# Input projection of a hybrid attention block: dense weights and tokens as fp16 halves with scales found on the chip

## The chip, the cores and the metric

The kernel runs on one core of one Trainium2 chip. The metric is the device time of one execution in microseconds (us). The kernel before has a median of 585.36 us over 2 runs (585.01 and 585.7).

The engines are named as in the profile: PE does matmuls and PEld its weight loads, DVE is VectorE, ACT is ScalarE, POOL is GpSimd, and SP issues the DMAs.

## The reference, cut to what matters

```python
D_MODEL, SEQ, N_META = 1024, 512, 16        # 528 tokens: 16 meta tokens, then 512
MLA_HEADS = FOX_HEADS = 16                  # both branches are 1024 wide
...
u = rmsnorm(h, pre_norm_g[l])
proj = u @ w_in[l]                          # [528, 1024] @ [1024, 7600]
(cq, ckv, k_pe_raw, z_mla, fq, fk, fv, f_logit, z_fox, gate_a, gate_b) = jnp.split(proj, split_idx, axis=-1)
...
y_mla = (o_mla * jax.nn.silu(z_mla)) @ w_br_mla[l]
...
o_fox = causal_block_attention(fox_heads(fq), fox_heads(fk), fox_heads(fv), FOX_SCALE, cum)
y_fox = (o_fox * jax.nn.silu(z_fox)) @ w_br_fox[l]
mixed = (jax.nn.sigmoid(gate_a) * y_mla + jax.nn.sigmoid(gate_b) * y_fox) @ w_out[l]
h = h + rmsnorm(mixed, post_norm_g[l])
```

The case is about `u @ w_in`: 7168 of its 7600 output columns are `z_mla`, `fq`, `fk`, `fv`, `z_fox` and the two gates. The other 432 (`cq`, `ckv`, `k_pe_raw`, `f_logit`) are the small projections.

## The kernel before, in words

**Three products for one.** Every fp32 matrix product is made of two parts per operand. A high part is the operand in the type fp32r, a low part is what the high part leaves, and three matmuls are summed in PSUM: high weights by high tokens, high weights by low tokens, low weights by high tokens. The tokens are `uTh` and `uTl` (1024 rows as 8 blocks of 128 partitions, 528 columns).

**Units.** The dense part of `w_in` is cut into 56 units of 128 output columns: 8 each of `fq`, `fk` and `v` (`fv`), 16 of `z` (8 for each branch) and 16 of `pg` (the gates). A unit has 8 blocks of the contraction and three products for each. `z`, `fq` and `pg` have 24 matmuls of 512 columns; `fk` and `v` also take the meta tokens and have 24 matmuls of 272 and 24 of 256 columns.

For each unit one DMA brings 128x1024 of raw fp32 weights (`wraw`, 512 KB). ACT casts the high part (`w<-wraw`, L136), and `split_lo` (L105) subtracts it from the raw weights for the low part, on POOL for 43 units of this size and on DVE for the others (`low[0]` names the engine).

**Stages.** After a preamble of some 59 us (tokens normed and transposed, small projections `psm`, first `fq` and `fk`) come 16 attention stages, one for two heads of a branch, FoX and MLA in turn; a FoX stage and the MLA stage after it are a pair here. Each stage computes scores (`st`), turns them on ACT and DVE into probabilities (`sf`, `pn`; L795, L830, L869), transposes these by DMA (`pt`), and multiplies them with the values of the stage before (`ov`). Between these PE works off a list called `fill`, which prepares the next stages:

- in a FoX stage (a z-stage below): the two `z` units of the pair, the first whole, the second in pieces between `mq`, `mk` and `v` of the next MLA stage;
- in an MLA stage (an fq-stage below): `fq`, `fk` and `v` of the next FoX stage.

PE's order is written out by hand (`tc.manual_schedule`). The other engines take an order from the tile framework's priorities, fixed when the program is built. After the last stage, at about 395 us, the merge begins: nine of the gates, the two branch projections and the output projection, with POOL idle.

**What consumes a unit.** `hl_done` (L251 on ACT, L105 on DVE) splits `fq` and `fk` into `hlq` and `hlk`. `z_unit` takes a tanh on ACT and L746 on DVE (`sil`). `v_unit` finds a scale for each partition (L710 to L720), and makes `vh`. `gate_unit` takes a tanh.

## Time and profile before

| what | value |
|---|---|
| median of the runs | 585.36 us (585.01, 585.7) |
| the profiled execution's own time | 585.71 us |
| its span, first to last instruction | 583.5 us |
| mean granted TensorE clock | 0.999 |
| busy time of PE, DVE, ACT, POOL | 574.2, 414.5, 356.4, 200.7 us |

The span has 2.2 us less than the execution's time. Busy time is a sum over stages that differ; a stage has to be read by its own window. A row of the timeline gives the start of an instruction in us from the span's start, its duration, engine, line, operation, output and inputs, shapes and a count, and in brackets the idle time before it and what ended that. A row of the groups gives the count, the busy time in us and the mean duration in ns. A matmul's duration reaches from its start until its last result is written, and the next matmul starts long before that, so the pace of PE is the distance of starts and not the duration.

### The profile page before, as it was taken

To read this page: it belongs to the slowest core of one execution; us is meant where nothing else is said; L and a number is where in the kernel's file an instruction comes from. 1 tells how busy PE (TensorE), PEld (TensorE's weight loads), DVE (VectorE), ACT (ScalarE), POOL (GpSimd) and SP (SyncE) were. 2 spreads that over 40 slices of the span, in tenths; PEclk is the share of its full clock that TensorE was granted. 3 is DMA by queue.
4 is the path that set the end of the run, shared out by engine and by line. 5 is a ranking of instruction groups with operands and counts; after the bars stand their busy time and mean duration, and the time that the engine had idled before them with its cause. 6 is when DMAs were issued, how large, how long until landed. Compare 5 with 4: busy or idle time off the path is not lost.

```text
span 583.5 us, 11105 instructions
## 1 busy us (share of the span) xinstructions
PE 574.2 (98%) x3841; PEld 496.5 (85%) x3841; DVE 414.5 (71%) x1156; ACT 356.4 (61%) x816; POOL 200.7 (34%) x270
## 2 busy tenths in 40 slices
PE   8999999999999999999999999999999999999995
PEld 6989889889889888888898898878998998888884
DVE  5854876884775775767758748895747876468967
ACT  7856774884774775767748747944343462443762
POOL 4317835464468472654544634520000000000000
PEclk9999999999999999999999999999999999999999
DMA  9535699999978999988987978977722534332603
GB/s 293 119 88 151 125 189 218 234 184 269 175 167 158 231 192 215 220 164 208 186 175 182 216 158 147 184 168 259 210 73 72 145 105 132 89 110 88 237 0 144
DMA packets 219999, 97.46 MB, mean 167 GB/s; under 512 B 131456, under 2 KB 209672, under 8 KB 219944
## 3 DMA queue, kind: packets, MB, share of 16 engines
q1 hardware_dynamic: 219944, 96.77, 71.2%
q8 instruction: 30, 0.49, 0.3%
q14 instruction: 25, 0.20, 0.1%
HBM read 62.36 MB, written 3.97 MB: 114 GB/s over the span
## 4 chain that ended last, share of the span: by engine, by line
PE 93%; ACT 2%; DMA 2%; issue 1%; POOL 1%; SPq 0%; DVE 0%; DVEq 0%; ACTq 0%; POOLq 0%
PE z L99 17%; PE pg L99 15%; PE v L99 9%; PE fk L99 8%; PE fq L99 8%; PE x L99 8%; PE py L99 7%; PE st L99 7%; PE ov L99 5%; PE psm L99 3%; PE y L99 2%; PE mq L99 2%; DMA pt<-pn 1%; PE ppe L99 1%; DMA wsr<-in_w_in_dram 1%; PE mk L99 1%
## 5 line engine op out<-in xcount | busy, mean ns | idle before, releaser
L105 POOL TENSOR_TENSOR w<-wraw,w 128x1024 fp32r<-128x1024 f32 (+2 forms) x61 | 118.6, 1951 | 113.8 <-ACT w L136 81.5
L136 ACT CAST w<-wraw 128x1024 fp32r<-128x1024 f32 (+1 forms) x72 | 74.6, 1041 | 48.5 <-PE py L99 19.7
L99 PE MATMUL z<-uTh,w 128*128 128x512 f32 x256 | 85.0, 393 | 0.0
L99 PE MATMUL pg<-uTh,w 128*128 128x512 f32 x256 | 80.7, 391 | 0.0
L830 ACT ACTIVATE sf<-sf,nb 128x272 f32<-128x272 f32 (+3 forms) x128 | 72.7, 569 | 11.5 <-DVE nb L795 10.6
L105 DVE TENSOR_TENSOR w<-wraw,w 128x512 fp32r<-128x512 f32 (+1 forms) x55 | 51.6, 949 | 27.9 <-ACT w L1125 20.0
L869 DVE SCALAR_TENSOR_TENSOR pn<-sf,ri,pn 128x512 f16<-128x512 f32 (+3 forms) x128 | 69.6, 609 | 1.6 <-ACT pn L865 1.5
L865 ACT ACTIVATE pn<-sf,ri 128x128 f16<-128x128 f32 (+3 forms) x128 | 59.7, 548 | 0.5 <-DVE ri L835 0.5
L99 PEld LDWEIGHTS pg<-uTh,w 128*128 128x128 f32 x256 | 48.1, 188 | 10.2 <-issue 0.3
L99 PEld LDWEIGHTS z<-uTh,w 128*128 128x128 f32 x256 | 48.1, 188 | 10.2
L99 PE MATMUL z<-uTl,w 128*128 128x512 f32 x128 | 50.1, 391 | 0.0
L99 PE MATMUL pg<-uTl,w 128*128 128x512 f32 x128 | 49.9, 390 | 0.0
L99 PE MATMUL fk<-uTh,w 128*128 128x272 f32 (+1 forms) x256 | 48.5, 283 | 0.0
L99 PE MATMUL v<-uTh,w 128*128 128x272 f32 (+1 forms) x256 | 47.5, 283 | 0.0
L99 PE MATMUL fq<-uTh,w 128*128 128x512 f32 x128 | 42.0, 398 | 0.0
L99 PE MATMUL st<-hlk,hlq 64*128 64x272 f32 (+4 forms) x480 | 41.2, 299 | 0.0
L710 DVE TENSOR_REDUCE vsc<-v 128x1 f32<-128x272 f32 (+1 forms) x32 | 13.2, 433 | 39.5 <-PE v L99 39.5
L99 PEld LDWEIGHTS fk<-uTh,w 128*128 128x128 f32 x256 | 40.4, 188 | 0.3
L99 PEld LDWEIGHTS v<-uTh,w 128*128 128x128 f32 x256 | 40.0, 188 | 0.1
L99 PE MATMUL py<-gh,w 128*128 128x512 f32 x128 | 39.7, 389 | 0.0
L99 PEld LDWEIGHTS st<-hlk,hlq 64*128 64x128 f32 x480 | 33.1, 186 | 4.1 <-ACT vh L729 2.8
L99 PE MATMUL v<-uTl,w 128*128 128x256 f32 (+1 forms) x128 | 36.2, 283 | 0.0
(255 smaller groups left out, 1332.1 us busy)
## 6 DMA issues: line engine op xcount, KB each, us to landing
wraw<-in_w_in_dram SPq DMA_DIRECT2D x56, 512.0 KB, 4.8
cbp<-c_dram SPq DMA_DIRECT2D x16, 264.0 KB, 4.0
wraw<-in_w_br_fox_dram SPq DMA_DIRECT2D x8, 512.0 KB, 4.2
tb<-in_w_out_dram SPq DMA_DIRECT2D x8, 512.0 KB, 5.4
wraw<-in_w_br_mla_dram SPq DMA_DIRECT2D x8, 512.0 KB, 4.2
wraw<-in_w_out_dram SPq DMA_DIRECT2D x6, 512.0 KB, 4.2
xr<-in_x_dram SPq DMA_DIRECT2D x4, 512.0 KB
out_dram<-yo SPq DMA_DIRECT2D x8, 256.0 KB, 2.0
```

The source lines that it names most:

```text
L99: nc.tensor.matmul(*a, **k)
L105: return eng.tensor_tensor(out=lo, in0=src, in1=f32(hi), op=ALU.subtract)
L136: nc.scalar.copy(wh[:, :n], raw[:, :n])
L710: nc.vector.tensor_reduce(out=sc[:, i : i + 1], in_=ps, op=ALU.max, axis=AX.X, apply_absolute_value=True)
L830: exps[b // 3] = nc.scalar.activation(sf, sf, AF.Exp, bias=sums["nb"][:, h, b : b + 1], scale=-1.0, accum_out=sums["su"][:, h, b : b + 1]).ins
L865: normed[:] = [nc.scalar.activation(hi, sf, AF.Copy, scale=rib).ins]
L869: nc.vector.scalar_tensor_tensor(out=lo, in0=sf, scalar=rib, in1=hi, op0=ALU.mult, op1=ALU.subtract)
```

## The change

**Tokens.** `pre_norm_g` is multiplied by a power of two from its largest magnitude, and the tokens are split into fp16 halves `hTh` and `hTl`. The factor is taken out again by constants in `su`, by which POOL also rescales `rt` and `gq` (128x320 and 128x384). The small projections still run as fp32r: for the first two token tiles POOL makes `hTh` and `hTl` from `uTh` and `uTl` (`narrowed`: a CAST of 128x1024 and two TENSOR_TENSOR of 128x1024 per tile), for the last two it makes `uTh` and a copy of `uTl` (`widened`: 8 CASTs of 128x512).

**Weights.** Each of the 56 units gets a scale. `peak` is a DVE reduction of the raw 128x1024 to a maximum of magnitude per partition. For each set of one to three units, a PE matmul of these maxima against a constant 128x128 tile (`spread`) gives a bound on every partition, and DVE takes the power of two out of it by bit operations (L195) and a reciprocal (L197), and POOL the factor back (L198). There are 24 such matmuls for the sets and one more for the tokens. Then ACT writes the high half with that scale (one instruction per unit, as the cast was). The low half is one DVE instruction for 10 units; for 46 units it is two POOL instructions, a TENSOR_SCALAR of raw times scale (L237, two operations, the second times 1.0) and the subtraction (L238).

**Consumers** undo the scales in instructions that were there already (an activation's scale, a `scalar_tensor_tensor` in place of a `tensor_tensor`), with two more 128x1 POOL instructions per stage.

**Order.** The units are built earlier, since a set's scale comes ahead of the first of its weights: a z-stage finds the scales of the three units `fq`, `fk`, `v` of the next fq-stage, an fq-stage those of the two `z` units of the next pair. Two buffers for raw weights are added, and loads are issued a stage earlier. `gT` and the sums of the merge move to rooms that the tokens leave.

```diff
-SC_FOX = 1.0 / math.sqrt(HD)
+SC_FOX = 4.0 / math.sqrt(HD)
...
+    spread = const.tile([128, 128], BF16, tag="spread", name="spread")
+    nc.gpsimd.memset(spread, 2.0 ** -14)
...
+    def scales(ws):
+        st = {}
+        def peak(j):
+            raw = ws[j].load()[1]
...
+            mp = st["sc"][:, 0:2].bitcast(BF16)[:, j : j + 1]
+            tc.keep_in_program_order(nc.vector.tensor_reduce(out=mp, in_=raw, op=ALU.max, axis=AX.X, apply_absolute_value=True))
+        def run_():
...
+            for w in ws:
+                w.peak()
+            sc, n = st["sc"], len(ws)
+            ps = scale_bank[0](f"scale{uid[0]}")[:, 0:n]
+            mm(ps, spread, sc[:, 0:2].bitcast(BF16)[:, 0:n], start=True, stop=True)
+            t, inv, r = (sc[:, o : o + n] for o in (3, 7, 11))
+            with tc.high_priority(offset=200):
+                nc.vector.tensor_scalar(out=t.bitcast(I32), in0=ps.bitcast(I32), scalar1=0x7F800000, scalar2=0x00800000,
+                                        op0=ALU.bitwise_and, op1=ALU.bitwise_or)
+                nc.vector.reciprocal(inv, t)
+                nc.gpsimd.tensor_scalar(out=r, in0=t, scalar1=su[:, 5:6], scalar2=1.0, op0=ALU.mult, op1=ALU.mult)
...
+    class Halved:
...
+        def __call__(self):
...
+            self.scale()
+            u, raw, parts, n = self.ld
...
+                nc.scalar.activation(hi, raw, AF.Copy, scale=self.s)
...
+                if low[0] is nc.vector:
+                    nc.vector.scalar_tensor_tensor(out=lo, in0=raw, scalar=self.s, in1=hi, op0=ALU.mult, op1=ALU.subtract)
+                else:
+                    whole_ = f32(room[:, 1024:2048])
+                    nc.gpsimd.tensor_scalar(out=whole_, in0=raw, scalar1=self.s, scalar2=1.0, op0=ALU.mult, op1=ALU.mult)
+                    nc.gpsimd.tensor_tensor(out=lo, in0=whole_, in1=hi, op=ALU.subtract)
...
     def u_act(k):
-        return uTh[:, k, :], uTl[:, k, :]
+        return hTh[:, k, :], hTl[:, k, :]
...
-    def win_w(off, i, up=0):
-        return weights(lambda: [win[:, :, off + 128 * i : off + 128 * i + 128]], lambda w: by_k(w[0], KD), up)
+    def win_w(off, i, room=None):
+        return Halved(lambda: win[:, :, off + 128 * i : off + 128 * i + 128], room)
...
-                za, zb = z_unit(1, pr), z_unit(0, pr)
-                fill = (vts[br, pr] if pr else begun) + za + q + zb[:3] + k + zb[3:5] + v + zb[5:]
+                za, zb = zs[pr]
+                q, k, v = feeds[si + 1]
+                fill = (vts[br, pr] if pr else begun) + za + q + zb[:3] + k + zb[3:5] + v + call(ws[0].scale, ws[0]) + zb[5:] + call(ws[1])
+                fill += loads_of(sets[si + 1])
...
-                fill = vts[br, pr] + q + k[:KD] + v + k[KD:]
+                    fill = vts[br, pr] + q + k[:KD] + v[:4] + call(ws[0].scale, ws[0]) + v[4:] + k[KD:] + call(ws[1]) + loads_of(sets[si + 1])
+                middles.append([sets[si - 1][2]])
...
                 n1()
+                for w in sets[si]:
+                    w.peak()
```

How this moves instructions on the engines is shown at three places. The first is DVE in a z-stage, after the scaled probabilities (`pn`). The row of numbers at the end is the output's shape. Before:

```order
L869 SCALAR_TENSOR_TENSOR pn_714<-sf_3161,ri_3159,pn_714 128x4x128
L746 SCALAR_TENSOR_TENSOR sil_3303<-sil_3303,z_3256 128x512
L105 TENSOR_TENSOR hlq_3320<-mq_3313,hlq_3320 128x512
L105 TENSOR_TENSOR hlk_3355<-mk_3351,hlk_3355 128x272
L105 TENSOR_TENSOR hlk_3355<-mk_3358,hlk_3355 128x256
L710 TENSOR_REDUCE vsc_3374<-v_3370 128x1
```

Now, at the same place (L1022 is the old L869, L897 the old L746, L855 the old L710):

```order
L1022 SCALAR_TENSOR_TENSOR pn_785<-sf_3333,ri_3331,pn_785 128x4x128
L182 TENSOR_REDUCE sc_3509<-wraw_3323 128x1
L897 SCALAR_TENSOR_TENSOR sil_3473<-sil_3473,z_3426 128x512
L182 TENSOR_REDUCE sc_3509<-wraw_3325 128x1
L109 TENSOR_TENSOR hlq_3489<-mq_3482,hlq_3489 128x512
L182 TENSOR_REDUCE sc_3509<-wraw_3327 128x1
L109 TENSOR_TENSOR hlk_3523<-mk_3519,hlk_3523 128x272
L109 TENSOR_TENSOR hlk_3523<-mk_3526,hlk_3523 128x256
L855 TENSOR_REDUCE vsc_3542<-v_3538 128x1
L195 TENSOR_SCALAR sc_3509<-scale_3560 128x3
```

Three peaks (L182) now stand between `pn` and `hlk`, and L195 reads what PE made of them.

The second place is PE in the same z-stage, after `v` of the MLA stage that follows and ahead of the last piece of the second `z` unit. Before:

```order
L99 MATMUL v_3376<-cTl,w_3306 128x256
L99 MATMUL v_3376<-cTh,w_3306 128x256
L99 MATMUL z_3329<-uTh,w_3324 128x512
L99 MATMUL z_3329<-uTl,w_3324 128x512
L99 MATMUL z_3329<-uTh,w_3324 128x512 x2
```

Now:

```order
L103 MATMUL v_3544<-cTl,w_3477 128x256
L103 MATMUL v_3544<-cTh,w_3477 128x256
L103 LDWEIGHTS spread
L103 MATMUL scale_3560<-sc_3509,spread 128x3
L103 LDWEIGHTS w_3319
L103 MATMUL z_3493<-hTh,w_3319 128x512
```

The scale matmul is new here; where `z` followed `v` directly, it now stands behind a matmul that reads the three peaks.

The third place is POOL between the end of a z-stage and the middle of the next fq-stage, where it makes the low parts of `fq`, `fk` and `v`. Before:

```order
L105 TENSOR_TENSOR w_3512<-wraw_3254,w_3512 128x1024
L105 TENSOR_TENSOR w_3569<-wraw_3311,w_3569 128x1024
L720 TENSOR_SCALAR vsc_3374<-vsc_3374 128x1
L105 TENSOR_TENSOR w_3623<-wraw_3327,w_3623 128x1024
L850 TENSOR_TENSOR mt_3587<-sf_3408,ri_3406 128x32
```

Now (L1003 is the old L850):

```order
L198 TENSOR_SCALAR sc_3509<-sc_3509,su 128x3
L237 TENSOR_SCALAR w_3565<-wraw_3323,sc_3509 128x1024
L869 TENSOR_SCALAR vsc_3542<-vsc_3542 128x1
L237 TENSOR_SCALAR w_3582<-wraw_3325,sc_3509 128x1024
L238 TENSOR_TENSOR w_3565<-w_3565 128x1024
L903 TENSOR_SCALAR vsc_3542<-sc_3185,vsc_3542 128x1
L237 TENSOR_SCALAR w_3735<-wraw_3327,sc_3509 128x1024
L238 TENSOR_TENSOR w_3582<-w_3582 128x1024
L238 TENSOR_TENSOR w_3735<-w_3735 128x1024
L1003 TENSOR_TENSOR mt_3766<-sf_3594,ri_3592 128x32
```

The low half of `fq` (`w_3565`) is finished by the fifth of these instructions, behind the first steps of `fq` and of `fk`; that of `fk` is finished after the first step of `v`.

## The prediction, as it was put on record

> **What bounds the kernel now.** I read the page first, then the chain of waits, then the groups by shape, and last the timeline of one pair of stages in the middle of the program.

> ```profile
> span 583.5 us, 11105 instructions
> PE 93%; ACT 2%; DMA 2%; issue 1%; POOL 1%; SPq 0%; DVE 0%; DVEq 0%; ACTq 0%; POOLq 0%
> ```

> ```profile
> 226.20:244.30 18.10, 18.10 (x123) 14.75 (x122) 14.47 (x57) 14.25 (x35) 7.93 (x11) 1.00 0.98 221
> 244.30:267.00 22.70, 22.70 (x197) 20.67 (x196) 14.23 (x48) 13.89 (x35) 12.73 (x19) 1.00 0.89 187
> 400.00:450.00 50.00, 50.00 (x308) 44.98 (x307) 30.27 (x47) 18.98 (x34) 0.00 (x0) 1.00 0.53 159
> ```

> ```profile
> PE psm L99 <- POOL wsh L306: 0.5, 1, 0.5
> ```

> The chain is PE for 93% of the span. The windows (after each window's length: PE, PEld, DVE, ACT, POOL, clock, DMA share, GB/s) show a z-stage, the fq-stage after it, and a piece of the merge. PE has no gap in any of them and a granted clock of 1.00. So the time is the sum of PE's steps, and the change counts in two ways: how much shorter a step becomes, and whether PE now has to wait. DVE is busy 14.47 of 18.10 us in the z-stage, the least room that any engine has there beside PE.

> **PE's steps.** A step is the distance of starts.

> ```profile
> 208.99 0.50 PE L99 MATMUL fq<-uTh,w 128*128 128x512 f32 x1
> 209.33 0.39 PE L99 MATMUL fq<-uTl,w 128*128 128x512 f32 x1
> ...
> 214.12 0.39 PE L99 MATMUL fq<-uTl,w 128*128 128x512 f32 x1
> ...
> 214.57 0.29 PE L99 MATMUL fk<-uTh,w 128*128 128x272 f32 x1
> ...
> 217.61 0.29 PE L99 MATMUL v<-uTh,w 128*128 128x272 f32 x1
> ```

> ```profile
> L99 PE MATMUL z<-uTh,w 128*128 128x512 f32 x256 | 85.0, 393 | 0.0
> L99 PE MATMUL fk<-uTh,w 128*128 128x272 f32 x128 | 25.6, 289 | 0.0
> L99 PE MATMUL fk<-uTh,w 128*128 128x256 f32 x128 | 23.1, 276 | 0.0
> L99 PE MATMUL ov<-pt,vp 128*64 128x512 f16 x96 | 13.1, 379 | 0.0
> L99 PE MATMUL ov<-pt,vp 128*64 128x256 f16 x96 | 7.9, 273 | 0.0
> ```

> Between the two rows of `fq<-uTl` lie 21 steps in 4.79 us: 228 ns for 512 columns in fp32r. Between `fk` and `v` lie 24 steps in 3.04 us: 127 ns for 272. A step is thus 162 to 165 ns shorter than the mean duration of the same form (393 less 228, 289 less 127); for 256 columns I take 276 less 163, 113 ns. No fp16 matmul with 128x128 weights is in this trace; the nearest are those of `ov`, with 64 columns of weights. Less 164, they give 215 ns for 512 columns and 109 for 256, and by their slope (106 ns over 256 columns) 116 for 272. So a step gains 13, 11 and 4 ns. There are 40 units of `z`, `fq` and gates with 24 matmuls of 512 (960), and 16 of `fk` and `v` with 24 of each half (384 and 384): 12.5 + 4.2 + 1.5 = **18.2 us gained**. The lower bound is no gain, if the weight load that now stands before each matmul shows; the upper one is the slope alone without any overhead (212, 113 and 106 ns): 15.4 + 5.4 + 2.7 = 23.5 us.

> **The scale matmuls.** There are 25, of one to three columns. What one costs is mostly the change of operands: the first `fq` after `ov` (208.99 above) takes 0.34 us to the next start, 0.11 more than the others. I take 0.13 us each, **3.2 us lost** in all, with bounds of 0.06 (little more than a step) and 0.25 (a change before and one behind).

> **The wait that the change adds.** In a z-stage PE's scale matmul stands behind `v`, and reads three peaks that DVE makes between `pn` and `hlk`. Behind it PE's last nine `z` matmuls are queued, and then the next stage's scores. PE's place and DVE's, with the rows that price a peak:

> ```profile
> 226.19 2.25 PE L99 MATMUL st<-hlk,hlq 64*128 64x272 f32 x30
> ...
> 242.15 0.39 PE L99 MATMUL z<-uTh,w 128*128 128x512 f32 x1
> ...
> 244.31 0.64 PE L99 MATMUL st<-hlk,hlq 64*128 64x272 f32 x6
> ...
> 249.81 0.50 PE L99 MATMUL fq<-uTh,w 128*128 128x512 f32 x1
> ```

> ```profile
> 234.09 4.09 DVE L869 SCALAR_TENSOR_TENSOR pn<-sf,ri,pn 128x512 f16<-128x512 f32 x8 [0.22 <-ACT pn L865]
> 238.10 0.68 DVE L746 SCALAR_TENSOR_TENSOR sil<-sil,z 128x512 f32<-128x512 f32 x1
> 239.00 0.69 DVE L105 TENSOR_TENSOR hlq<-mq,hlq 128x512 fp32r<-128x512 f32 x1 [0.22 <-ACT hlq L251]
> ```

> ```profile
> L710 DVE TENSOR_REDUCE vsc<-v 128x1 f32<-128x272 f32 x16 | 7.1, 442 | 21.1 <-PE v L99 21.1
> L105 DVE TENSOR_TENSOR w<-wraw,w 128x1024 fp32r<-128x1024 f32 x27 | 32.8, 1219 | 7.9 <-ACT w L136 7.9
> L351 DVE TENSOR_SCALAR hn<-ht,st 128x1024 f32<-128x1024 f32 x3 | 2.7, 887 | 0.1
> ```

> The stage begins at 226.19 and `v` is over at 242.15, 15.96 us in; 39 `z` matmuls ahead of it gain 0.51, so PE asks for the scale at 15.45. DVE is done with `pn` at 238.18, 11.99 us in, since the scores that start it don't get faster. The only reduction in the trace (442 ns for 272 elements) has about the time of a two-input pass of that width, and such a pass over 1024 elements takes 1.22 us; I price a peak at that. Peak, `sil`, peak, `hlq`, peak are then 3 x 1.22 + 0.68 + 0.69 = 5.03 us, less some 0.1 of overlap at each (eight `pn` have it too), so 16.5. PE waits about **1.1 us**, in seven z-stages 7.7 us. With a peak at the 0.89 us of L351 the wait is nil; with late DMAs or peaks at 1.5 us it is 2. What covers the peaks elsewhere: an fq-stage has 8.5 us of DVE idle, the merge 20 of 50, and there I cost them at nothing; were that cover gone, two peaks of an fq-stage would be 2.4 us. The last stage makes three peaks (the last gates) with PE arriving 1.9 us sooner than they do by the same count: 1.9 us. ACT writes the high halves in as many instructions as it cast them, and DMAs carry the same bytes: nothing for both, as long as the five raw buffers fill a stage early.

> **The preamble.** POOL, idle there before but for the casts of `wsh`, now narrows and widens the tokens.

> ```profile
> 10.71 0.91 POOL L306 CAST wsh<-wsr 128x864 fp32r<-128x864 f32 x1 [0.27 <-DMA wsr<-in_w_in_dram]
> 11.59 2.08 POOL L310 TENSOR_TENSOR wsl<-wsr,wsh 128x864 fp32r<-128x864 f32 x1
> ```

> A CAST of 128x1024 goes in ahead of the third `wsh` (0.9 us), for which PE waited already (0.5 us above). Then four subtractions of 2 us and the rescaling of `rt` and `gq` stand before the `uTh` that PE's third tile reads, about 24 to 26 us in, where PE comes at 25: I take 1.1 more, so **2.0 us lost** (0 to 5).

> **The low halves on POOL.** One subtraction becomes a scaling and a subtraction.

> ```profile
> L105 POOL TENSOR_TENSOR w<-wraw,w 128x1024 fp32r<-128x1024 f32 x43 | 104.6, 2434 | 84.6 <-ACT w L136 81.5 <-DMA pt<-pn 2.8
> L306 POOL CAST wsh<-wsr 128x864 fp32r<-128x864 f32 x3 | 2.8, 926 | 7.1 <-DMA wsr<-in_w_in_dram 7.1
> L523 POOL TENSOR_SCALAR fa<-fT 16x528 f32<-16x528 f32 x1 | 2.0, 1994 | 12.3 <-ACT fT L440 12.3
> L720 POOL TENSOR_SCALAR vsc<-vsc 128x1 f32<-128x1 f32 x16 | 3.4, 215 | 4.5 <-DVE vsc L716 4.5
> ```

> The price T of the scaling has ends far apart. By the one-input CAST it is 1.1 us (926 ns over 864 elements, 1024 here). By L523, the same operation with two steps, it is (1994 - 215) / 528 = 3.37 ns an element, 3.7 us. What can be borne: the third peak is 16.5 us into the z-stage; with the matmul, L195 and L198 POOL begins at 17.3, and the low half of `fq` comes after two scalings and a subtraction, at 19.9 + 2T with the 128x1 in between. The z-stage now lasts 18.12 - 0.62 + 0.13 + 1.1 = 18.7, `fq` starts 5.5 later and its third matmul reads the low half at 24.7. So up to T = 2.4 us nothing waits. Per pair POOL has 20.7 us by the windows; five scalings at 1.1 and 1 us of small ones make 27 of some 41. L523 is the nearest in kind, the CAST in shape and in having a plain stream of one input on all partitions; L523 uses a maximum as its second step, and a single record on 16 partitions. I take the CAST's side, not by much.

> [...]

> **The sum.** 18.2 - 3.2 - 7.7 - 1.9 - 2.0 = 3.4 us gained. The profiled execution took 585.71 us, 2.2 more than its span, so 582.3; the median before is 0.35 below that execution, so **582 us**. With half the way to each bound of these terms as a likely error (9 us up and 2.6 down for the steps, 1.5 and 0.9 for the matmuls, 3 and 3.9 for the waits, 1.5 and 1 for the preamble), put together by their squares, it lies between 577 and 592.

> **Rivals.**

> 1. *PE doesn't wait for the scales.* If a peak costs 0.9 us or less, as L351 does, the third one is there before PE: the 9.6 us come back, 572.4 us. For it: DVE has 3.6 us idle in a z-stage. Against it: the three peaks have to lie in the 3.5 us between `pn` and the end of `v`, and the idle time lies mostly after that.
> 2. *POOL's scaling runs at L523's rate and POOL becomes the bound* (the slower side). With T = 3.7 the low half of `fq` comes at 27.3, 2.6 us late; that of `fk`, another scaling and subtraction behind, at 33.6, where PE arrives at 32.3, 1.3 late. That is 3.9 us in seven stages, 27 us, and some 5 in the preamble, where the first `fq` stands behind two scalings: 614 us. It decides from T = 2.4 and costs over 2% from about T = 3.0. For it: the only record of this operation. Against it: the CAST's 1.07 ns an element.
> [...]

> **How the numbers follow.** My forecast has 0.48, the first rival 0.19, the second 0.31, the third 0.02. The range of the forecast alone is 577 to 592. To leave no more than 0.2 outside, the range reaches to both rivals: 572 to 614. A difference of 2% (573.7 to 597.1) is about what a measurement of this kernel tells from no change. Faster than that: two thirds of the first rival, the third, and a little of the forecast, 0.17. Slower: nearly all of the second, 0.30. Within: 0.53.

> **What would show it.** Right: `z` steps of 215 ns; waits of PE on DVE's L182 of about 1 us in each z-stage, none in the merge; POOL's L237 near 1.1 us and busy about two thirds of a pair. Wrong: a mean of L237 above 2.4 us with PE waiting for `w` from POOL at `fq`; no PE waits on L182; `z` steps of 228 ns, which would leave 600 us; or PE waiting on raw weights from a DMA.

## The result, and the profile after

The changed kernel takes 644.86 us (median of 643.93 and 645.78) where the kernel before takes 585.36: a ratio of 1.102, with a 95% interval of 1.094 to 1.109. That is 59.5 us slower, outside the range on record (572 to 614), where the forecast of 582 was a small gain. The profiled execution took 643.93 us. First the page's span and busy times, then the waits of PE over the whole span (total, times, longest).

```profile
span 642.2 us, 11395 instructions
...
PE 583.9 (91%) x3866; PEld 402.2 (63%) x3866; DVE 501.8 (78%) x1261; ACT 366.1 (57%) x816; POOL 288.3 (45%) x383
```

```profile
PE scale L103 <- DVE sc L182: 39.9, 17, 7.2
PE ppe L103 <- ACT w L148: 5.5, 1, 5.5
```

Two things are new: PE waits 39.9 us for the peaks (L182), and the granted clock, 0.999 before, has dents (mean 0.962). The windows of a z-stage, the fq-stage after it and a piece of the merge answer to the three of before (after the length: PE, PEld, DVE, ACT, POOL, clock, DMA share, GB/s).

```profile
310.93:329.60 18.67, 17.71 (x125) 10.57 (x125) 17.69 (x63) 11.97 (x32) 6.36 (x13) 1.00 1.04 203
329.60:355.90 26.30, 23.88 (x200) 17.22 (x199) 19.04 (x53) 16.71 (x38) 20.53 (x27) 0.94 0.80 153
450.00:500.00 50.00, 50.00 (x327) 33.90 (x326) 38.87 (x55) 21.31 (x34) 6.19 (x5) 1.00 0.69 217
```

The z-stage is 0.57 us longer than before, the merge piece has no gap, and the fq-stage went from 22.70 to 26.30 with PE idle for 2.42. The loss thus has three places. In the table, idle is the length less PE's busy time, and the clock loss is the sum of busy time times (1 - granted clock) over windows of 1 us; the rest is what remains of the difference.

| part | before | after | difference | of it idle | of it clock | rest |
|---|---|---|---|---|---|---|
| up to the first stage | 59.0 | 80.6 | +21.6 | +14.3 | +6.1 | +1.1 |
| first to last stage's start | 307.7 | 338.8 | +31.0 | +30.2 | +9.2 | -8.4 |
| from there to the end | 216.7 | 222.8 | +6.1 | +4.5 | +2.9 | -1.2 |

Of the 39.9 us that PE waits at the scale matmuls, 6.4 lie ahead of the first stage, 17.2 in the eight z-stages, 12.0 in the fq-stages and 4.3 in the last stage.

**What the steps did.** Rows of PE in the z-stage (its wait, 327.54), of `v` and of `z`, and the groups that answer to the prices of the forecast:

```profile
327.54 0.16 PE L103 MATMUL scale<-sc,spread 128*128 128x3 bf16 x1 [0.96 <-DVE sc L182]
...
343.69 0.28 PE L103 MATMUL v<-hTl,w 128*128 128x272 f16 x1
...
344.73 0.28 PE L103 MATMUL v<-hTl,w 128*128 128x272 f16 x1
...
347.48 0.16 PE L103 MATMUL scale<-sc,spread 128*128 128x2 bf16 x1 [2.36 <-DVE sc L182]
347.51 0.28 PE L103 MATMUL v<-hTh,w 128*128 128x272 f16 x1
...
418.19 0.38 PE L103 MATMUL z<-hTl,w 128*128 128x512 f16 x1
...
418.84 0.38 PE L103 MATMUL z<-hTl,w 128*128 128x512 f16 x1
```

```profile
L182 DVE TENSOR_REDUCE sc<-wraw 128x1 bf16<-128x1024 f32 x47 | 55.8, 1207 | 0.0
L237 POOL TENSOR_SCALAR w<-wraw,sc 128x1024 f32<-128x1024 f32 x46 | 54.5, 1186 | 5.4 <-PE v L103 3.8 <-DVE vsc L858 1.1 <-issue 0.6
```

Three `z` steps in 0.65 us are 217 ns, nine `v` steps in 1.04 are 116, and a scale matmul holds the next one back by 30 ns. A peak takes 1.21 us, POOL's scaling 1.19.

**What an fq-stage waits for.** The stage starts at 329.60. In the order of time, from the timelines of ACT, POOL, DVE and PE:

```profile
331.60 2.20 ACT L231 ACTIVATE w<-wraw,sc 128x1024 f16<-128x1024 f32 x2
333.68 0.52 ACT L983 ACTIVATE sf<-sf,nb 128x272 f32<-128x272 f32 x1
334.98 4.23 POOL L238 TENSOR_TENSOR w<-w 128x1024 f16<-128x1024 f32 x2
337.06 2.17 DVE L987 TENSOR_SCALAR su<-su 128x2 f32<-128x2 f32 x1 [0.90 <-ACT sf L983]
340.27 0.75 DVE L1022 SCALAR_TENSOR_TENSOR pn<-sf,ri,pn 128x512 f16<-128x512 f32 x1
341.17 4.00 DVE L1022 SCALAR_TENSOR_TENSOR pn<-sf,ri,pn 128x128 f16<-128x128 f32 x7 [0.15 <-DMA QP<-qpe_dram]
345.09 2.33 DVE L182 TENSOR_REDUCE sc<-wraw 128x1 bf16<-128x1024 f32 x2
```

And the same three places of before, in a stage that starts at 244.30:

```profile
246.46 0.52 ACT L830 ACTIVATE sf<-sf,nb 128x272 f32<-128x272 f32 x1 [0.38 <-DVE nb L795]
250.12 0.17 DVE L834 TENSOR_SCALAR su<-su 128x2 f32<-128x2 f32 x1 [0.41 <-ACT sf L830]
252.21 4.41 DVE L869 SCALAR_TENSOR_TENSOR pn<-sf,ri,pn 128x512 f16<-128x512 f32 x8
```

`sf` starts 4.1 us into the stage instead of 2.2, behind the last two high halves on ACT. L987, a DVE step over two elements a partition that took 0.17 us, now takes 2.17 and ends at 339.23, 0.02 us after POOL's two subtractions (339.21). `pn` ends 15.6 us into the stage instead of 12.3. Only then come two peaks of 1.2 us, while PE is at the scale matmul at 345.12: 2.36 us of waiting.

**What the wait does to the clock.** In the windows behind it the clock is 0.50, and `v` steps take 228 ns (three from 348.12 to 348.80):

```profile
348.00:349.00 1.00, 1.00 (x6) 0.65 (x5) 0.73 (x4) 0.14 (x1) 0.34 (x2) 0.50 1.14 212
...
350.00:351.00 1.00, 1.00 (x6) 0.69 (x5) 0.44 (x1) 0.01 (x1) 0.90 (x2) 0.50 1.08 213
351.00:352.00 1.00, 1.00 (x10) 0.85 (x9) 0.00 (x0) 0.00 (x0) 1.00 (x1) 0.90 1.10 196
```

That is 3.4 us at half speed, another 1.7 us. The z-stage's wait of 0.96 us is followed by none.

**One long wait.** Four of the eight z-stages wait 0.96 to 1.05 us at the scale matmul, the others 1.60, 2.06, 2.41 and 7.20. The longest ends at 284.23, in the stage that starts at 261.39, and the length of the peaks isn't its cause. From ACT's timeline:

```profile
268.63 0.40 ACT L756 CAST w<-wraw 128x256 fp32r<-128x256 f32 x1 [6.66 <-DMA wraw<-in_w_uq_dram]
...
270.29 0.52 ACT L983 ACTIVATE sf<-sf,nb 128x272 f32<-128x272 f32 x1
```

In ACT's order the cast of the raw weights of another projection (`w_uq`) stands ahead of `sf`, and its load comes late: SP issued it at 265.86, 4.5 us into the stage. So `sf` starts 8.9 us into the stage instead of 1.9, the peaks come that much later, and the stage lasts 26.8 us, 8.1 more than the z-stage above. In the kernel before, the load for the stage at 226.19 was issued at 205.15, and no engine waited for these loads. Whether the raw buffers or the new order of the loads moved it is not shown.

### The profile page after: what moved, and what is told of

Read it like the earlier page. It is cut to its first block, busy times and chain, and to the rows that moved or that the text cites. A ratio compares the mean times of both kernels' runs of the same rounds, so it can differ in the third digit from the quotient of the medians.

```text
span 642.2 us, 11395 instructions
## 1 busy us (share of the span) xinstructions
PE 583.9 (91%) x3866; PEld 402.2 (63%) x3866; DVE 501.8 (78%) x1261; ACT 366.1 (57%) x816; POOL 288.3 (45%) x383
## 5 line engine op out<-in xcount | busy, mean ns | idle before, releaser
L103 PEld LDWEIGHTS <-w 128*128 128x128 f16 x1728 | 168.7, 100 | 162.8 <-issue 45.8
L231 ACT ACTIVATE w<-wraw,sc 128x1024 f16<-128x1024 f32 x47 | 53.2, 1149 | 104.4 <-DVE sc L197 61.2
L238 POOL TENSOR_TENSOR w<-w 128x1024 f16<-128x1024 f32 x46 | 100.8, 2202 | 0.7
L198 POOL TENSOR_SCALAR sc<-sc,su 128x2 f32<-128x2 f32 (+2 forms) x24 | 8.9, 371 | 187.0 <-DVE sc L195 182.7
L103 PE MATMUL z<-hTh,w 128*128 128x512 f16 x256 | 84.1, 390 | 0.0
L103 PE MATMUL pg<-hTh,w 128*128 128x512 f16 x256 | 79.9, 388 | 0.0
L1022 DVE SCALAR_TENSOR_TENSOR pn<-sf,ri,pn 128x512 f16<-128x512 f32 (+3 forms) x128 | 71.1, 617 | 3.3 <-ACT pn L1018 2.8
L237 POOL TENSOR_SCALAR w<-wraw,sc 128x1024 f32<-128x1024 f32 x46 | 54.5, 1186 | 5.4 <-PE v L103 3.8
L182 DVE TENSOR_REDUCE sc<-wraw 128x1 bf16<-128x1024 f32 x47 | 55.8, 1207 | 0.0
L103 PE MATMUL v<-hTh,w 128*128 128x272 f16 (+1 forms) x256 | 50.1, 292 | 0.0
L103 PE MATMUL z<-hTl,w 128*128 128x512 f16 x128 | 49.8, 389 | 0.0
L103 PE MATMUL pg<-hTl,w 128*128 128x512 f16 x128 | 49.6, 388 | 0.0
L109 DVE TENSOR_TENSOR w<-wraw,w 128x512 fp32r<-128x512 f32 (+1 forms) x42 | 35.8, 864 | 11.9 <-ACT w L148 6.0
L103 PE MATMUL scale<-sc,spread 128*128 128x2 bf16 (+2 forms) x24 | 4.0, 167 | 39.9 <-DVE sc L182 39.9
```

The lines of the kernel that those rows point to most:

```text
L103: nc.tensor.matmul(*a, **k)
L109: return eng.tensor_tensor(out=lo, in0=src, in1=f32(hi), op=ALU.subtract)
L182: tc.keep_in_program_order(nc.vector.tensor_reduce(out=mp, in_=raw, op=ALU.max, axis=AX.X, apply_absolute_value=True))
L198: nc.gpsimd.tensor_scalar(out=r, in0=t, scalar1=su[:, 5:6], scalar2=1.0, op0=ALU.mult, op1=ALU.mult)
L231: nc.scalar.activation(hi, raw, AF.Copy, scale=self.s)
L237: nc.gpsimd.tensor_scalar(out=whole_, in0=raw, scalar1=self.s, scalar2=1.0, op0=ALU.mult, op1=ALU.mult)
```

## The experiments

The kernels of a group share their runs of the kernel before (585.2 to 585.8 us). Ratios are to it.

**e2: shorter peaks.** The peak reads 64 of the 1024 columns, so the scales come from a part of the weights; the order, the matmuls and the buffers stay.

```diff
-            tc.keep_in_program_order(nc.vector.tensor_reduce(out=mp, in_=raw, op=ALU.max, ...
+            tc.keep_in_program_order(nc.vector.tensor_reduce(out=mp, in_=raw[:, 0:64], op=ALU.max, ...
```

> The changed kernel, with each peak taken over 64 of the 1024 raw columns (the other 960 are left out of the maximum); everything else stays. Theory (DVE's time for the peaks, and what is queued around them, makes PE wait): the 56 peaks cost 0.2 us instead of 1.2, the waits at the scale matmuls fall from 40 us to under 10, the clock loss from 18 to under 8, and the time is about 600 us. Rival (the scale waits for raw weights or for its own chain through PE, DVE and POOL): the waits stay above 25 us and the time above 630 us.

616.40 us, 1.053 (1.048 to 1.058): 28 us less. PE's waits:

```profile
PE scale L103 <- DVE sil L897: 4.7, 1, 4.7
...
PE scale L103 <- DVE sc L182: 3.0, 5, 1.9
```

The waits on L182 fall from 39.9 to 3.0 us and the clock loss from 18.2 to 10.0. (The 4.7 us are one more wait at a scale matmul, in the z-stage whose `w_uq` comes late.) Most z-stages are at 17.6 to 19.0 us and most fq-stages at 22.0 to 22.6. From the first to the last stage's start, 23.4 of the lost 31.0 us come back, so the peaks' length is the bulk of the loss in the stages; the first stage still starts 18.6 us late. The waits fell as the theory said; the time stayed 16 us above the 600 that it gave.

**e5: without L987.** It is dropped, with the constant that it divides by set to 1.

```diff
-PSCALE = 512.0
+PSCALE = 1.0
...
-                nc.vector.tensor_scalar(out=su, in0=su, scalar1=1.0 / PSCALE, scalar2=None, op0=ALU.mult)
```

> The changed kernel without the instruction L987 (the probabilities lose their factor of 512; nothing else changes). In the run with L987 as a scalar_tensor_tensor it still stood 2.15 us behind POOL's L238, so the form was not it. [...] Rival (L987 stood for a reason of its own): pn starts 2 us sooner, and the time is under 628 us.

636.76 us, 1.088 (1.086 to 1.090). In the fq-stage that starts at 328.03, from the timelines of POOL, DVE and PE:

```profile
333.40 4.23 POOL L238 TENSOR_TENSOR w<-w 128x1024 f16<-128x1024 f32 x2
335.49 0.17 DVE L987 RECIPROCAL ri<-su 128x2 f32<-128x2 f32 x1 [0.89 <-ACT sf L983]
337.45 4.16 DVE L1021 SCALAR_TENSOR_TENSOR pn<-sf,ri,pn 128x512 f16<-128x512 f32 x8
343.92 0.16 PE L103 MATMUL scale<-sc,spread 128*128 128x2 bf16 x1 [0.36 <-DVE sc L182]
```

The reciprocal (now L987) runs in 0.17 us in the midst of POOL's subtractions, and such a stage lasts 22.6 instead of 26.3 us, with 0.36 us of waiting and no clock loss. So the 2 us that L987 stands are a link of the chain. With it 2.0 us of the wait went. `pn` still ends 13.6 us into the stage and not 12.3, behind the later `sf`. The total gains only 8.1 us, and stays above the rival's 628, because z-stages lose the gain again: those of 20.6, 23.3 and 28.6 us start `sf` 4.8, 5.8 and 10.9 us in, and ACT's waits for the loads of `w_uq` sum to 18.9 us (9.8 in the changed kernel). The waits on L182 sum to 30.5.

**e1: L987 in another form**, with a second operand that doesn't change the result.

```diff
-                nc.vector.tensor_scalar(out=su, in0=su, scalar1=1.0 / PSCALE, scalar2=None, op0=ALU.mult)
+                nc.vector.scalar_tensor_tensor(out=su, in0=su, scalar=1.0 / PSCALE, in1=su, op0=ALU.mult, op1=ALU.min)
```

> The changed kernel, with the small DVE instruction L987 (su times a constant, 128x2 and 128x6) written as a scalar_tensor_tensor instead of a tensor_scalar; nothing is left out. [...] Then L987 is under 0.25 us everywhere, the waits at the scale matmul in the fq-stages fall from 2.4 to 0.5 us, the clock losses behind them go too, and the time is about 630 us. Rival (DVE is short of time by the peaks themselves): L987 finishes sooner, but the waits stay above 1.5 us in the fq-stages and the time above 640 us.

642.86 us, 1.098 (1.093 to 1.103), the waits on L182 at 40.0 us:

```profile
L987 DVE SCALAR_TENSOR_TENSOR su<-su 128x2 f32<-128x2 f32 x16 | 17.2, 1076 | 14.0 <-ACT sf L983 13.5
```

The mean over 16 is 1.08 us (1.04 before the edit): it stands just as long. The 630 us on record rested on the author's guess that the one form of operation was to blame, and that fell. A peak that ran beside one of POOL's subtractions in the changed kernel (at 205.87, beside L109) took 1.21 us, as the others did.

**e6: two high halves later**, that of `fk` asked for in the middle of the fq-stage, so that ACT should come to `sf` sooner.

```diff
-... + call(ws[0].scale, ws[0]) + zb[5:] + call(ws[1])
+... + call(ws[0].scale, ws[0]) + zb[5:]
...
-                middles.append([sets[si - 1][2]])
+                middles.append([sets[si - 1][1], sets[si - 1][2]])
```

> The changed kernel with the halves of fk asked for one place later in program order, in the middle of the fq-stage with those of v, and no longer at the end of the z-stage; nothing is left out. Then one ACT pass less (1.15 us) stands ahead of the exponentials of the fq-stage, and POOL's L238 of fk and v come after the masks. Theory (ACT's passes and POOL's collision together make the fq-stage's peaks late): exponentials start 1 us sooner, L987 takes 0.2 us, the waits at the fq-stages' scale matmul fall from 2.4 to under 1 us unless pn now meets L238, and the time is 622 to 636 us. Rival (the place of ACT's passes does not matter): the waits stay at 2 us or more, and the time stays within 5 us of 645.

647.88 us, 1.107 (1.105 to 1.109): no gain, 39.2 us of waits on L182. The edit misses its aim: two high halves still stand ahead of `sf` in such an fq-stage, `sf` still starts 4.1 us in, and L987 stands as long (a mean of 1.03 us over 16, 1.04 before the edit). What an earlier `sf` would give is thus not tested.

**e3: the scale matmuls at the end of PE's stage**, behind everything else that it has there.

```diff
-... + v + call(ws[0].scale, ws[0]) + zb[5:] + call(ws[1])
+... + v + zb[5:] + call(ws[0].scale, ws[0]) + call(ws[1])
...
-... + v[:4] + call(ws[0].scale, ws[0]) + v[4:] + k[KD:] + call(ws[1]) + ...
+... + v + k[KD:] + call(ws[0].scale, ws[0]) + call(ws[1]) + ...
```

> The changed kernel, with the scale matmul one place later in PE's order: in a z-stage behind the whole second z unit instead of ahead of its last nine matmuls, in an fq-stage behind v and fk instead of in the middle of v. Nothing is left out. Theory (the place of the scale matmul makes the wait): DVE's peaks come 1 to 2.4 us late for the old place and in time for the new one, so the waits at L182 fall under 0.3 us in the stages, the clock stays at 1.00 there, and the time is about 610 us, since the halves of the next units still come in time. Rival (the wait only moves): PE waits 1 to 3 us for the high or low halves at fq and z of the next stage instead, and the time stays above 635 us.

660.86 us, 1.129 (1.118 to 1.139).

```profile
PE scale L103 <- DVE sc L182: 20.6, 9, 5.1
PE st L103 <- DVE sc L195: 19.8, 14, 2.7
```

Half of the wait went to the next stage's scores, whose bank L195 still reads, and the clock loss rose to 28 us. A later place on PE doesn't take the wait away. It only moves, as the rival said, though not to the place that the rival named.

**e4: eight extra matmuls ahead of the scale in fq-stages**, which fill the wait and whose result is overwritten.

```diff
+            for _ in range(warmth[0]):
+                mm(bank_, hTh[:, 0, 0:128], hTh[:, 0, 0:512], start=True, stop=True)
```

> The changed kernel, with eight matmuls of 512 columns on tokens (1.7 us of PE work whose result is overwritten) put ahead of the scale matmul in the fq-stages; the rest is the same. Theory (the slow clock follows PE's idle time): where PE waited 2.4 us it now works for 1.7 of them, the waits at L182 fall to 0.7 us there, the granted clock stays at 1.00 behind them, and the 1.7 us lost per slow stretch come back; against it stand some 4 us of extra work in the stages that hardly waited, so the time is 638 to 645 us with no clock below 0.95 behind the scale matmuls of the fq-stages. Rival (the clock falls for another reason, such as the load of the chip at these places): the slow stretches stay where they are, and the time is above 650 us.

642.68 us, 1.098 (1.095 to 1.101). The fq-stage that answers to the one above lasts 24.6 us instead of 26.3, though PE is at the scale no sooner (17.9 us in), and the clock behind it is 1.00: that 1.7 us are the clock. The window behind its scale matmul, at 350.04:

```profile
350.06:353.06 3.00, 3.00 (x28) 2.62 (x28) 1.67 (x5) 1.15 (x1) 1.73 (x3) 1.00 1.13 211
```

The total gains only 2 us: three fq-stages that had waited little got 0.8 to 1.7 us longer by the extra work, and the z-stage with the late load now waits 8.4 us.

**e8: fixed scales**, 2^11, with no peaks, no scale matmuls and no steps of DVE and POOL on them; the scales aren't taken from the data. All else stays: POOL's two instructions, the tokens, the buffers, the order.

```diff
-            for w in ws:
-                w.peak()
-            sc, n = st["sc"], len(ws)
...
+            for w in ws:
+                w.s, w.r = fix["fix"][:, 0:1], fix["fix"][:, 1:2]
```

> The changed kernel with a fixed scale for the weights of all units (2 to the 11th, written once): the 56 peaks, the 24 scale matmuls and the DVE and POOL steps behind them are left out; POOL's two passes for a low half, the tokens' narrowing and widening, the order of the units and the loads stay. Theory (the scales' peaks and their place on PE are most of the loss in the stages, the tokens and raw buffers most of that in the preamble): against the run with short peaks the waits for L182 go, the preamble keeps some 10 us of its loss, and the time is 595 to 606 us. Rival (POOL's longer low halves and what they meet on DVE keep the loss): 612 us or more, as with the short peaks.

600.66 us, 1.026 (1.023 to 1.029). The stages take 304.5 us together, 3.3 less than before, and the undisturbed pair 17.5 + 21.6 = 39.1. So finding the scales costs 44 us, 34 of them between the first and the last stage's start. What is left is above all the preamble, 20.6 us late. The late loads are left too (ACT waits 15.6 us for `w_uq`). PE's longest waits:

```profile
PE psm L103 <- POOL uTh L479: 7.6, 2, 7.1
PE ov L103 <- DMA pt<-pn: 7.2, 4, 3.0
PE ppe L103 <- ACT w L148: 4.1, 1, 4.1
```

**e9, e10, e11: the preamble.** e9 runs the small projections on the fp16 halves of the tokens (weights as an fp16 and a bf16 half), so that POOL neither narrows nor widens. e10 shifts the rule for the two added raw buffers, so that the load that feeds `ppe` finds a free one. e11 has both.

```diff
-                for q, (u, w) in enumerate(((uTh, wsh), (uTl, wsh), (uTh, wsl))):
+                for q, (u, w) in enumerate(((hTh, wsh), (hTl, wsh), (hTh, wsl))):
...
-        narrowed(0)
-        narrowed(1)
```

```diff
-        elif more[0] is not None and loads[0] % 5 > 2:
+        elif more[0] is not None and (loads[0] + 2) % 5 > 2:
```

> The small projections run on the fp16 halves of the tokens (weights as an fp16 and a bf16 half), so that POOL neither narrows nor widens a token; the scales, the peaks and the stages stay as in the changed kernel (644.9 us). The question is what makes the first stage start 21.5 us later. Theory A: POOL's token work, for which the small projections wait, is most of it (with the scales taken away the stage still started 20.8 us late, with 7.6 us of waits on POOL's uTh). Then the stage starts 8 to 13 us earlier, of which 1.6 are shorter steps of the small projections: 632 to 637 us, and no wait on POOL is left ahead of the first fq. Rival B: the two DVE peaks that stand behind the low halves of the tokens, and the late load for ppe, decide: then the waits on DVE's L182 (4.0 and 2.5 us) and for ppe (5.5 us) stay, and the time falls by under 4 us.

> One number: the rule that says which loads go to the two added raw buffers is shifted by two, so that the two loads after the preamble's five (a w_in unit and the one that feeds ppe) find a free buffer instead of one that is held until a scale and both halves are made; the later loads shift with them. Theory B (in part): the wait of 5.5 us for ppe comes from the load that stands in SP's queue behind one that waits for a buffer. Then that wait is gone or under 1 us, and the first stage starts 4 to 6 us earlier: 639 to 641 us. Rival: the load is late for another reason (the queue itself, or the casts behind it), the wait stays, 644 to 645 us.

> Both edits together. If POOL's token work and the held buffer are separate causes, their gains add up (12 to 18 us, 627 to 633 us), and the first stage starts at most 5 us later than in the kernel before, which is then what the two scales in the preamble cost with the clock behind them. If one only covers the other, the time is that of the better one alone.

637.34, 645.39 and 639.52 us (1.089, 1.103 and 1.092, each within 0.005). The first stage starts at 74.9, 80.0 and 74.7 us instead of 80.6. e9 gains 5.7 us there, less than theory A had; some 1.6 of them are the shorter steps of the small projections (96 steps of 198 ns became 183), so POOL's tokens cost about 4. The held buffer costs next to nothing, and the two gains don't add up to the 12 us or more that e11 was to show. In the rows of e11 and e12 shown here the line numbers lie one lower than in the changed kernel. In e11 the raw weights for `ppe` were asked for at 19.5 us, and yet PE, ACT and POOL show:

```profile
58.33 0.50 PE L102 MATMUL ppe<-cTh,w 128*128 128x512 f32 x1 [2.58 <-ACT w L147]
61.46 1.22 PE L102 MATMUL ppe<-cTh,w 128*128 128x512 f32 x2 [2.40 <-POOL w L108]
...
52.75 1.15 ACT L230 ACTIVATE w<-wraw,sc 128x1024 f16<-128x1024 f32 x1 [1.12 <-DVE sc L196]
57.67 0.60 ACT L147 CAST w<-wraw 128x512 fp32r<-128x512 f32 x1
55.02 5.16 POOL L237 TENSOR_TENSOR w<-w 128x1024 f16<-128x1024 f32 x2
60.15 1.26 POOL L108 TENSOR_TENSOR w<-wraw,w 128x512 fp32r<-128x512 f32 x1
```

**e12: e11 with the halves of `ppe` asked for first**, ahead of those of the first `fv` and gate, which need a scale.

```diff
-        early[0]()
...
-        early[1]()
...
+        pe0[0][1].prep()
+        for w in early:
+            w()
         run(pe0)
```

> The kernel with both preamble edits (639.5 us; the first stage starts 15.7 us later than in the kernel before), and the halves of the first fv and the first gate are asked for behind those of the unit that feeds ppe, instead of ahead of them; nothing else differs. What made ppe wait there was neither a load nor POOL's tokens: with its raw weights long in place ppe still waited 2.6 us for ACT and 2.4 us for POOL, and the granted clock was 0.50 to 0.61 behind. Theory: ACT's cast and POOL's subtraction for ppe stand in their queues behind the halves of fv and gate, which wait for the scale, which waits for DVE's peaks and behind a DVE step that waits for ACT. Then both waits and the clock loss behind them go, and the first stage starts 6 to 10 us earlier: 630 to 634 us. Rival: the wait only passes to fv, whose low half now comes after ppe's: a wait of 2 to 4 us on POOL's L237 or ACT's L230 ahead of v, the clock drops there, and under 3 us are gained (636.5 us or more).

634.30 us, 1.082 (1.079 to 1.086). PE's waits up to 92 us:

```profile
PE scale L102 <- DVE sc L181: 5.4, 2, 3.0
PE z L102 <- POOL w L237: 2.5, 1, 2.5
```

Both waits of `ppe` are gone, and the first stage starts at 64.4, 10.3 us sooner than in e11. What is late there is 5.3 us, about the two waits for scales (5.4) and 1.6 of clock less the shorter steps. Half of the 10.3 us is lost again: a new wait of 2.5 us on POOL, and the first two stages last 49.3 us instead of 45.6.

**e7: halves without scales.** The kernel before, with the tokens as fp16 halves, and the weights of the 56 units and of the small projections as an fp16 high and a bf16 low half; every other line stays, so POOL has one subtraction for a unit. It has no protection for weights outside fp16's range, which the change has.

```diff
+        if half:
+            wh, wl = wh.bitcast(F16)[:, 0:1024], wl.bitcast(BF16)[:, 0:1024]
```

> The kernel before, with tokens as two fp16 halves, and the weights of the input projection (the small one too) as an fp16 high half and a bf16 low half: no scales, no peaks, no rescaling, the same instructions in the same order as the kernel before, only other types (the low half in bf16 keeps 8 bits below the fp16 half). Theory (fp16 steps bring their whole gain, and everything lost comes from finding the scales and from the work around them): 960 steps of 512 gain 12 ns, 384 of 272 gain 11, 384 of 256 gain 4, some 96 of 432 in the small projection gain 14, 18.6 us, so 567 us and PE without waits. Rival (fp16 matmuls themselves lose what they gain, by their weight loads or by the change between types): 578 us or more.

571.24 us, 0.975 (0.973 to 0.977): faster than both, and 4 us above the 567 expected. The windows of a pair, PE without a gap:

```profile
302.00:319.51 17.51, 17.51 (x126) 10.68 (x124) 15.00 (x59) 13.93 (x34) 6.94 (x12) 1.00 0.93 183
319.51:341.10 21.59, 21.59 (x197) 16.03 (x195) 13.64 (x46) 14.20 (x37) 12.43 (x19) 1.00 0.89 202
```

A pair is 39.10 us instead of 40.80. The profiled execution (573.25 us) has 4.6 us of idle PE in other stages, most of it waits for DMAs, and 1.7 of clock loss. From the first stage on it is 11.4 us shorter than before; without the added idle time (4.3) and the clock, the steps of the 56 units are worth some 17 us, near the forecast's 18.2.

## Why the prediction was wrong, by its own steps

- **PE's steps: right.** 215, 116 and 109 ns were forecast; 217, 116 and (from the median of steps) 109 came. e7 shows the gain: 14 us net, and some 17 for the steps of the 56 units alone, without the waits that it has elsewhere.
- **The scale matmuls: too dear**, 0.13 us each forecast, 0.03 measured: 0.7 us instead of 3.2.
- **The z-stage: right where nothing else comes late.** Forecast 1.1 us of waiting and 18.7 us of length; measured 0.96 and 18.67. The peak at 1.22 us was right (1.21), and so the first rival fell. But only four of the eight z-stages are so. The term stood at 7.7 us, for seven stages, and came out at 17.2: one wait of 7.20 goes back to the load of `w_uq`, and for loads the forecast had "nothing for both, as long as the five raw buffers fill a stage early".
- **POOL's scaling: right**, 1.19 us for 1.1. The second rival fell: a plain product by two scalars doesn't run at the rate of L523, whose like in the changed kernel (L656) still takes 1.99 us for 528 elements.
- **The step that failed: "What covers the peaks elsewhere: an fq-stage has 8.5 us of DVE idle, the merge 20 of 50, and there I cost them at nothing."** An idle total says nothing about when. Of these 8.5 us, 5.0 lie behind the point where PE asks for the scale (15.5 us into the stage), and 1.3 ahead of the end of `pn`. By the rows of before `pn` ended 12.3 us into the stage; two peaks make 14.7; PE asks at 15.5. The margin was 0.9 us, and `pn` came 3.3 later: 2.0 by L987, which stands behind POOL's longer work (0.17 us became 2.17, and e5 gives 2.0 back), and 1.3 by the later `sf` behind ACT's halves (what e5 leaves). The price that the forecast named for a lost cover, 2.4 us, is what the undisturbed fq-stages show (2.36), but it stood in no case.
- **No term for the clock.** A wait of 2.36 us cost another 1.7 where the clock halved behind it; all drops together cost 18.2 us.
- **"The preamble ... 2.0 us lost (0 to 5)": failed**, 21.6. The forecast counted POOL's tokens as far as `uTh`. The runs show three causes, one on the other: POOL's tokens (about 4 us, e9), the halves of `ppe` queued on ACT and POOL behind halves that wait for a scale (10.3, e12), and the waits for two scales with the clock behind them (5.4 and 1.6 in e12).
- **The last stage**: 1.9 us forecast; 4.34 of waiting and 2.9 of clock there.
- Steps should have given back some 17 us in the changed kernel, and the column "rest" has 8.5. The other half is not settled: it is spread over many short gaps and steps, and no single row carries it.

## What to carry to other kernels

A value that one engine must find before another may go on makes a chain; price it by the moment when its last link can start, in every stage that has it, and not by the idle time of the stage. Ask which steps on that chain may stand until an engine that the change makes busier is done (here L987, 2.17 us instead of 0.17), what queue order puts work that needs no new value behind work that does, and which load comes late in the new order. A bottleneck engine that never waited may also lose speed after its first long waits: here PE's clock fell to 0.50 for 3.4 us behind a wait of 2.36.

## What the runs showed of the hardware that was not expected

**The clock after a wait.** Two fq-stages of e11 have the same wait for the scale, 2.34 and 2.35 us:

```profile
343.76 0.16 PE L102 MATMUL scale<-sc,spread 128*128 128x2 bf16 x1 [2.34 <-DVE sc L181]
...
388.67 0.16 PE L102 MATMUL scale<-sc,spread 128*128 128x2 bf16 x1 [2.35 <-DVE sc L181]
```

```profile
340.35:343.76 3.41, 1.07 (x10) 0.77 (x8) 3.41 (x5) 0.21 (x1) 0.69 (x2) 1.00 0.32 63
343.76:347.17 3.41, 3.41 (x17) 2.31 (x17) 1.69 (x5) 1.15 (x1) 2.12 (x3) 0.50 1.12 212
384.72:388.13 3.41, 1.60 (x14) 1.21 (x13) 3.41 (x6) 0.74 (x2) 1.22 (x3) 1.00 0.29 57
388.13:391.54 3.41, 2.87 (x27) 2.50 (x27) 2.23 (x6) 1.15 (x1) 1.59 (x3) 1.00 0.96 180
```

Behind the first PE does 17 matmuls in 3.41 us at a clock of 0.50; behind the second the clock stays at 1.00. The stages last 26.26 and 24.63 us.

**DVE beside POOL.** In the changed kernel L987 with two elements a partition, a TENSOR_SCALAR, stood until POOL's two-input pass (L238) was over in all nine stages where the two met (median 2.17 us instead of 0.17, its end 0.02 to 0.03 us after POOL's). As a SCALAR_TENSOR_TENSOR (e1) its mean over all 16 stages was 1.08 us, beside 1.04. A reciprocal of the same two elements ran in 0.17 us in the midst of such a pass (e5, at 335.49).
